# Latent heads of a streaming-encoder layer: the second pieces of long rows transposed on TensorE and split from PSUM, the first pieces' buffers placed in the chunked heads' V memory

## The chip, the cores and the metric

The kernel runs on one core of a Trainium2 chip. The metric is device time in microseconds (us), the median over runs; less is better. The engines are named as in the profile: PE (TensorE matmuls; PEld is its weight load), DVE (VectorE), ACT (ScalarE), POOL (GpSimd), SP (SyncE, which issues the DMAs here). The trace is that of one profiled execution.

## The reference

One layer over 1024 tokens of width 1024. What matters here is the attention with latent heads (eight of them), which comes after a chunked attention (eight more heads) and before the output projection and the gated MLP:

```python
def mla_attention(q, k, v):                      # q, k: 96 wide per head, v: 64 wide
    scale = Dq ** -0.5
    key_chunk = jnp.arange(S) // CHUNK           # CHUNK = 64
    def block(args):                             # Q_BLOCK = 128 queries
        qi, i = args
        s = jnp.einsum('bqhd,bkhd->bhqk', qi, k) * scale
        q_chunk = (i * Q_BLOCK + jnp.arange(Q_BLOCK)) // CHUNK
        s = jnp.where((key_chunk[None, :] <= q_chunk[:, None])[None, None], s, NEG_INF)
        p = jax.nn.softmax(s, axis=-1)
        return jnp.einsum('bhqk,bkhd->bqhd', p, v)
```

Row block i of a head (0 to 7) sees the keys of blocks 0 to i, so its probabilities are 128 x 128(i+1). The texts below number these rows 1 to 8: row n has 128n columns.

## The kernel before

Everything is fp32 in, fp32 out; products are made from pairs of a high and a low part (three matmuls for fp32r pairs in `gemm3`, L150 to L152; two fp16 halves for probabilities and V). The stages are: adaptive norm and the chunked heads' q and k, then attention, then the output projection, then the MLP (from about 752 us on). The change touches the attention stage alone, and there the latent heads, from about 430 to 680 us.

A head is handled as two units of four rows (`Unit`, `mla_unit`). A unit's `prep` makes its q page and k page in `qk_page` (L612 to L626): four PE transposes (L618) into a PSUM tile of the tag `T`, which has one buffer (`TB` = 1), then ACT writes the high part (L621 for q, L624 for k) and DVE the low part (L622, L625). The names in the trace are `mq_ps`, `mk_ps`, `mq`, `mk`.

`scores(i)` then makes one row: fp32r matmuls into one of two PSUM tiles `S` (L658, `sm`), a memset of the masked corner (L676) and the row's minimum (L677, `mm`) on DVE, the exponential with its sum on ACT (L683, `Pm`), the reciprocal and its scale on DVE (L685, L686, `rim`). Rows of more than 640 columns (rows 6, 7 and 8) are cut into a first piece of 512 columns and a second of 256, 384 or 512. For each piece POOL writes the high fp16 half into a buffer `hl` (L71), DVE the low half (L703), and SP issues a DMA transpose of both halves (L705) into `PT`. The tags `HL` and `PT` have three buffers each (`HL_BUFS`, `PT_BUFS`).

`values(i)`, three rows later (`DEPTH` = 3), multiplies the transposed halves with V (L716, `pvm`) into the PSUM tile `pv`; after four rows ACT and DVE make the output (L723, `sbm`; L724, `om`), and SP stores it.

Two things set the order of the work. The program text interleaves rows with pieces of other work ("fillers": the second latent group's q, k and V in `f_up`, and half of the output projection in `f_oca`, whose PE products are `oc` and whose loads are `cl` and `wor`), so many per row as `pace` asks for. And the scheduler reorders each engine's queue by priority: scores have an offset of 400, pieces 200, values 200. What it can't change is the order in which tiles of one tag get their buffers, which is that of the program text. The chunked heads' V lies in six buffers of the tag `v16` (`f_v`), of 2 KB a partition.

Of the kernel before, what the change touches and what calls it, by code (L numbers as in the profile page):

```python
# [12 lines left out]
F32 = mybir.dt.float32  # L13
F32R = mybir.dt.float32r
F16 = mybir.dt.float16
BF16 = mybir.dt.bfloat16
I32 = mybir.dt.int32
AF = mybir.ActivationFunctionType
# [3 lines left out]
MUL, ADD, SUB, MIN, MAX = ALU.mult, ALU.add, ALU.subtract, ALU.min, ALU.max  # L22

P = 128
# [16 lines left out]
P_BUFS, HL_BUFS, PT_BUFS, TB = 3, 3, 3, 1  # L41
# [21 lines left out]
def layer_kernel(ctx, tc, I, out):  # L63
    nc = tc.nc
    pe, act, dve, pool, sp = nc.tensor, nc.scalar, nc.vector, nc.gpsimd, nc.sync
# [4 lines left out]
    def scale_pool(o, i, s):  # L70
        pool.tensor_scalar(o, i, s, 1.0, op0=MUL, op1=MUL)  # L71
# [24 lines left out]
    ident = cst.tile([P, P], F32, name="ident")  # L96
# [27 lines left out]
    apg = att_pg.__enter__()  # L124
# [5 lines left out]
    ps = psA.__enter__()  # L130
# [12 lines left out]
    def pgtile(shape, dt, name):  # L143
        return apg.tile(shape, dt, name=name, tag="pg", bufs=6)
# [91 lines left out]
    for d in range(ND):  # L236
        if d + 1 < ND:
            load_ada(d + 1)
        w = wada[d]
# [15 lines left out]
        for t in range(NT):  # L255
            h, j = divmod(t, 4)
# [74 lines left out]
    at = att.__enter__()  # L331
# [296 lines left out]
    class Unit:  # L628
# [7 lines left out]
        def scores(u, i):  # L636
# [3 lines left out]
            lo = max(0, i - 4) if u.band else 0  # L640
            n = (i - lo + 1) * P
            nm = f"{u.nm}_{i}"
            rsum = cst.tile([P, 1], F32, name=f"rs{nm}", tag="rsum", bufs=4)
            ri = cst.tile([P, 1], F32, name=f"ri{nm}", tag="ri", bufs=4)
            with tc.high_priority(offset=OFF_S):
# [17 lines left out]
                if u.band:  # L663
                    if i >= 4:
                        dve.memset(sv[64:128, 0:64], BIG)
                    w = min(n, 256)
# [11 lines left out]
                pieces = [(0, n)] if n <= 640 else [(0, 512), (512, n)]  # L678
                if n <= 640:
                    pr = at.tile([P, 640], F32, name=f"P{nm}", tag="P", bufs=P_BUFS)  # L680
                else:
                    pr = pgtile([P, 1024], F32, f"P{nm}")
                act.activation(pr[:, :n], sv, AF.Exp, bias=m[:], scale=-1.0, accum_out=rsum[:, 0:1])  # L683
            with tc.high_priority(offset=OFF_P):
                dve.reciprocal(ri[:], rsum[:, 0:1])  # L685
                dve.tensor_scalar(ri[:], ri[:], PSCALE, None, op0=MUL)  # L686
                u.pt[i] = []
                for x, (p0, p1) in enumerate(pieces):
                    w = p1 - p0
                    hl = at.tile([P, 1280], F16, name=f"hl{nm}_{x}", tag="HL", bufs=HL_BUFS)  # L690
                    pp = pr[:, p0:p1]
                    cnt[0] += 1
                    mode = (MODE_C if u.band else MODE_M)[cnt[0] % 4]
                    if mode == "2":
                        scale_pool(pp, pp, ri[:])
                        act.activation(hl[:, :w], pp, AF.Copy)
                        pool.tensor_tensor(hl[:, w:2 * w], pp, hl[:, :w], op=SUB)
                    else:
                        if mode == "1":
                            scale_pool(hl[:, :w], pp, ri[:])  # L700
                        else:
                            act.activation(hl[:, :w], pp, AF.Copy, scale=ri[:])
                        dve.scalar_tensor_tensor(hl[:, w:2 * w], pp, ri[:], hl[:, :w], op0=MUL, op1=SUB)  # L703
                    tt = at.tile([P, 10, P], F16, name=f"PT{nm}_{x}", tag="PT", bufs=PT_BUFS)
                    sp.dma_start_transpose(tt[:, :2 * w // P, :], hl[:, :2 * w])  # L705
                    u.pt[i].append((tt, lo + p0 // P, w // P))
            return sum(3 * max(107, w / 2.4) for _, _, w, _ in segs)
# [109 lines left out]
    for n in range(len(tiles) + DEPTH):  # L817
        if n < len(tiles):
            u, i = tiles[n]
# [4 lines left out]
        if n >= DEPTH:  # L824
            u, i = tiles[n - DEPTH]
# [47 lines left out]
    for t in range(NT):  # L873
        lo = gb.tile([P, 4, P], F32R, name=f"ol{t}", tag="ol", bufs=3)
# [39 lines left out]
    def split(src, nm, tag="ws"):  # L914
        w = mt(tag, [P, 2, 512], nm, F32R)
        hi_of("a", w[:, 0], src)
        lo_of("p", w[:, 1], src, w[:, 0])
        return w
# [130 lines left out]
    for h in range(2):  # L1049
# [4 lines left out]
        for j in range(NF):  # L1054
# [3 lines left out]
            w = [split(raw[:, n * 512:(n + 1) * 512], f"wds{h}_{j}{n}") for n in range(2)]  # L1058
# [93 lines left out]
```

## Time and profile before

| what | value |
|---|---|
| median of 3 runs | 1462.71 us (1461.91 to 1462.82) |
| profiled execution, its own time | 1464.36 us |
| its span | 1462.2 us, mean granted clock 0.934 |
| busy PE, PEld | 1278.0 (87%), 1058.7 (72%) |
| busy DVE, ACT, POOL | 1013.6 (69%), 611.4 (42%), 823.0 (56%) |
| DMA transposes for latent heads | 88, 3.3 us from issue to landing (median) |
| DMA transposes for chunked heads | 64, 3.2 us |
| chain that ended last | PE 39%, DMA 17%, DVE 15%, POOL 13%, issue 12% |

Busy time is the sum of an engine's instructions; the shares are averages over stages with different limits. The chain is followed back from the last instruction, at each step to what released it; "issue" is time in which an engine waited for nothing that the profile shows. In a group's row the numbers after the bar are its busy time, the mean time of one in ns, and the idle time of the engine before them with what ended it. In a row of waits they are the total, the number of times and the longest. In the table of stretches a stretch's start and end come first, then its length, each engine's busy time, PE's granted clock, the DMA engines' busy share and the rate in GB/s.

### The profile page before, as it was taken

The page shows a single profiled execution, that of the slowest core. Times are in us where ns is not written, and L with a number is a line of the kernel's source. Part 1 is how long each engine was busy: PE and PEld are TensorE (multiplying, and loading weights), DVE is VectorE, ACT ScalarE, POOL GpSimd, SP SyncE. Part 2 cuts the span into 40 slices and gives each one's busy share as a digit, 9 for nine tenths or more (in the row PEclk, how much of TensorE's full clock was granted, in tenths as well). Part 3 has the DMA queues.
Part 4 walks back from the last instruction along what each step waited for, and adds up shares of the span by engine and source line. Part 5 has one row for each costly group of instructions (what it writes and reads, how often), then busy time and mean ns, then how long its engine had stood idle before and what let it go on. Part 6 is the DMA issues. An engine that isn't in the chain of part 4 may idle for free.

```text
span 1462.2 us, 20198 instructions
## 1 busy us (share of the span) xinstructions
PE 1278.0 (87%) x6836; PEld 1058.7 (72%) x6836; DVE 1013.6 (69%) x1734; ACT 611.4 (42%) x1190; POOL 823.0 (56%) x845
## 2 busy tenths in 40 slices
PE   3859989998967788885776999999999998999997
PEld 2759878886756666664655878788888887887885
DVE  6874776476667868872476887777777777566653
ACT  4453354243455545543274434344444433332331
POOL 5263554274599954534644555566655555665662
PEclk9979987999787899996887999999999999999998
DMA  7323647455522577879611322322222244446442
GB/s 281 134 71 74 131 114 148 129 119 120 112 52 51 115 163 156 180 142 253 246 72 59 105 110 101 116 87 87 87 87 83 75 140 164 151 144 238 146 142 101
DMA packets 218595, 185.94 MB, mean 127 GB/s; under 512 B 148086, under 2 KB 183034, under 8 KB 217468
## 3 DMA queue, kind: packets, MB, share of 16 engines
q1 hardware_dynamic: 218492, 184.66, 44.5%
q8 instruction: 54, 0.88, 0.3%
q14 instruction: 49, 0.40, 0.1%
HBM read 121.17 MB, written 28.84 MB: 103 GB/s over the span
## 4 chain that ended last, share of the span: by engine, by line
PE 39%; DMA 17%; DVE 15%; POOL 13%; issue 12%; ACT 3%; SPq 1%; DVEq 0%; POOLq 0%; ACTq 0%
POOL wds L82 5%; DMA aw<-w_ada 5%; PE p L924 4%; PE p L926 4%; PE p L925 4%; DMA wu<-w_up 3%; DMA PTm<-hlm 3%; PE sc L658 2%; PE dnp L1067 2%; PE dnp L1069 2%; PE dnp L1068 2%; PE sm L658 2%; DVE adacc L243 2%; DVE aacc L430 1%; DVE u L1002 1%
## 5 line engine op out<-in xcount | busy, mean ns | idle before, releaser
L82 POOL TENSOR_TENSOR wds<-wd,wds 128x512 fp32r<-128x512 f32 x88 | 154.6, 1777 | 99.0 <-ACT wds L75 99.0
L82 POOL TENSOR_TENSOR wc<-ws,wc 128x512 fp32r<-128x512 f32 x22 | 65.4, 2972 | 137.8 <-ACT wc L75 137.8
L1057 DVE TENSOR_TENSOR wd<-wd,gmbc 128x1024 f32<-128x1024 f32 x44 | 67.5, 1533 | 80.4 <-DMA wd<-w_down 80.4
L1069 PE MATMUL dnp<-wds,g 128*128 128x512 f32 x308 | 118.4, 390 | 4.5 <-DVE g L82 4.5
L1067 PE MATMUL dnp<-wds,g 128*128 128x512 f32 x308 | 119.6, 390 | 1.9 <-DVE xo L1075 1.9
L75 ACT ACTIVATE wds<-wd 128x512 fp32r<-128x512 f32 x88 | 54.8, 624 | 157.3 <-PE dnp L1069 152.2
L1068 PE MATMUL dnp<-wds,g 128*128 128x512 f32 x308 | 119.5, 389 | 0.0
L71 POOL TENSOR_SCALAR hlm<-Pm,rim 128x512 f16<-128x512 f32 (+4 forms) x88 | 61.9, 706 | 70.1 <-DMA PTm<-hlm 55.1
L703 DVE SCALAR_TENSOR_TENSOR hlm<-Pm,rim,hlm 128x512 f16<-128x512 f32 (+4 forms) x88 | 68.0, 777 | 30.1 <-POOL hlm L71 29.7
L71 POOL TENSOR_SCALAR hlc<-Pc,ric 128x640 f16<-128x640 f32 (+2 forms) x64 | 45.3, 710 | 76.9 <-DVE ric L686 41.2
L1015 DVE TENSOR_TENSOR ws<-wu,wu 128x512 f32<-128x512 f32 x22 | 30.7, 1396 | 76.2 <-DMA wu<-w_up 76.2
L82 DVE TENSOR_TENSOR g<-gr,g 128x512 fp32r<-128x512 f32 x44 | 71.9, 1635 | 11.5 <-ACT g L75 11.5
L1001 DVE SCALAR_TENSOR_TENSOR u<-c,pk,u 128x1023 f32<-128x1023 f32 x44 | 77.4, 1765 | 2.0 <-ACT u L1000 2.0
L1036 ACT ACTIVATE u<-u 128x1024 f32<-128x1024 f32 x22 | 23.4, 1063 | 132.1 <-DVE u L1002 132.1
L683 ACT ACTIVATE Pc<-sc,mc 128x640 f32<-128x640 f32 (+2 forms) x64 | 42.1, 659 | 82.5 <-DVE mc L673 62.0
L658 PE MATMUL sm<-mk,mq 96*128 96x512 f32 (+3 forms) x288 | 68.9, 372 | 7.9 <-ACT Pm L683 7.3
L1000 ACT ACTIVATE u<-c,pk 128x1024 f32<-128x1024 f32 x44 | 52.3, 1236 | 56.2 <-DVE c L1032 56.2
L716 PE MATMUL pvm<-PTm,vt 128*128 128x128 f16 x576 | 50.5, 242 | 28.8 <-DMA PTm<-hlm 24.3
L658 PE MATMUL sc<-k,q 64*128 64x512 f32 (+3 forms) x288 | 70.3, 372 | 4.9 <-ACT Pc L683 3.0
L430 DVE SCALAR_TENSOR_TENSOR aacc<-aw,cs,aacc 128x256 f32<-128x256 f32 x84 | 44.9, 535 | 40.6 <-DMA aw<-w_ada 40.0
L716 PEld LDWEIGHTS <-vt 128*128 128x128 f16 x576 | 41.1, 109 | 41.7 <-issue 38.3
L1069 PEld LDWEIGHTS dnp<-wds,g 128*128 128x128 f32 x308 | 57.8, 188 | 17.7 <-DVE g L82 5.7
(368 smaller groups left out, 4342.0 us busy)
## 6 DMA issues: line engine op xcount, KB each, us to landing
wu<-w_up SPq DMA_DIRECT2D x44, 512.0 KB, 4.3
wd<-w_down SPq DMA_DIRECT2D x44, 512.0 KB, 4.7
aw<-w_ada SPq DMA_DIRECT2D x96, 128.0 KB, 2.3
g_d<-u SPq DMA_DIRECT2D x22, 512.0 KB, 2.6
gr<-g_d SPq DMA_DIRECT2D x44, 256.0 KB, 3.7
x<-x SPq DMA_DIRECT2D x16, 512.0 KB, 8.3
adaw<-w_ada_a SPq DMA_DIRECT2D x8, 1024.0 KB, 5.5
wq_r<-w_qk SPq DMA_DIRECT2D x32, 128.0 KB, 2.6
```

What stands on the lines that cost most here:

```text
L71: pool.tensor_scalar(o, i, s, 1.0, op0=MUL, op1=MUL)
L82: (pool if eng == "p" else dve).tensor_tensor(o, i, f32(hi), op=SUB)
L430: dve.scalar_tensor_tensor(acc[:], w[:], cs[:, k:k + 1], acc[:], op0=MUL, op1=ADD)
L658: last = pe.matmul(s[:, c:c + w], qpg[rs_, a, q], kpgs[kh][rs_, b, ko:ko + w], start=(a == 0 and b == 0), stop=(a == 1))
L703: dve.scalar_tensor_tensor(hl[:, w:2 * w], pp, ri[:], hl[:, :w], op0=MUL, op1=SUB)
L716: last = pe.matmul(u.pv[:, c], u.vst(j), mov, start=(x == 0), stop=(x == len(todo) - 1))
L924: pe.matmul(pt, sh, pg[:, 0], start=(k == 0), stop=False)
L1001: dve.scalar_tensor_tensor(u[:, 1:], c[:, :S - 1], pk[:, cv + 1:cv + 2], u[:, 1:], op0=MUL, op1=ADD)
L1057: dve.tensor_tensor(raw[:], raw[:], gmbc[:], op=MUL)
L1067: pe.matmul(pts[t][n], sh, w[n][:, 0], start=(j == 0), stop=False)
L1068: pe.matmul(pts[t][n], sh, w[n][:, 1], start=False, stop=False)
L1069: pe.matmul(pts[t][n], sl, w[n][:, 0], start=False, stop=(j == NF - 1))
```

## The change

For rows 6, 7 and 8 of the latent heads the second piece no longer goes through `hl` and a DMA transpose. POOL scales the piece in place in fp32, PE transposes it in blocks of 128x128 into a tile of tag `T`, ACT copies the tile to the fp16 high half in `PT`, and DVE writes the low half as the difference of the tile and that half. The first piece of such a row keeps its way, but its `hl` and its `PT` come from the tag `v16`. Rows of up to 640 columns, and all rows of the chunked heads, are as before.

```diff
                 for x, (p0, p1) in enumerate(pieces):
                     w = p1 - p0
-                    hl = at.tile([P, 1280], F16, name=f"hl{nm}_{x}", tag="HL", bufs=HL_BUFS)
+                    if x:
+
+                        tt = at.tile([P, 10, P], F16, name=f"PT{nm}_{x}", tag="PT", bufs=PT_BUFS)
+                        nk = w // P
+                        scale_pool(pr[:, p0:p1], pr[:, p0:p1], ri[:])
+                        tp = ps.tile([P, 512], F32, name=f"tp{nm}", tag="T", bufs=TB)
+                        for j in range(nk):
+                            pe.transpose(tp[:, j * P:(j + 1) * P], pr[:, p0 + j * P:p0 + (j + 1) * P], ident[:])
+                        th = tt[:, :nk, :].rearrange("p a b -> p (a b)")
+                        act.activation(th, tp[:, :w], AF.Copy)
+                        dve.tensor_tensor(tt[:, nk:2 * nk, :].rearrange("p a b -> p (a b)"), tp[:, :w], th, op=SUB)
+                        u.pt[i].append((tt, lo + p0 // P, nk))
+                        continue
+                    if len(pieces) > 1:
+                        hl = apg.tile([P, 1024], F16, name=f"hl{nm}_{x}", tag="v16", bufs=6)
+                    else:
+                        hl = at.tile([P, 1280], F16, name=f"hl{nm}_{x}", tag="HL", bufs=HL_BUFS)
...
-                    tt = at.tile([P, 10, P], F16, name=f"PT{nm}_{x}", tag="PT", bufs=PT_BUFS)
+                    if len(pieces) > 1:
+                        tt = apg.tile([P, 8, P], F16, name=f"PT{nm}_{x}", tag="v16", bufs=6)
+                    else:
+                        tt = at.tile([P, 10, P], F16, name=f"PT{nm}_{x}", tag="PT", bufs=PT_BUFS)
                     sp.dma_start_transpose(tt[:, :2 * w // P, :], hl[:, :2 * w])
```

## The prediction

> **What bounds the kernel now.** First the cores' line: one core, mean granted clock 0.934, span 1462.2 us; the profiled execution itself took 1464.36, so 2.16 us lie around the span, and the execution is 1.65 above the median 1462.71. The change touches only rows of the latent heads, so the second view is the table of stretches, cut at the first exponential of each of the eight latent heads (L683, a row's 128 columns wide one):
>
> ```profile
> core 0: us, PE busy (x) PEld busy (x) DVE busy (x) ACT busy (x) POOL busy (x), PEclk, DMA share, GB/s
> 432.70:475.20 42.50, 30.32 (x157) 25.09 (x157) 31.63 (x87) 23.41 (x59) 40.34 (x74) 0.76 0.24 48
> 475.20:503.10 27.90, 20.25 (x126) 15.73 (x125) 24.20 (x63) 18.12 (x43) 26.78 (x46) 0.90 0.54 116
> 503.10:533.60 30.50, 27.63 (x166) 21.84 (x166) 21.79 (x48) 14.63 (x31) 21.01 (x26) 0.92 0.70 156
> 533.60:565.60 32.00, 25.44 (x174) 20.69 (x173) 21.54 (x53) 14.56 (x32) 12.99 (x17) 0.90 0.75 141
> 565.60:590.60 25.00, 21.41 (x149) 17.06 (x148) 21.08 (x52) 13.94 (x31) 14.15 (x15) 0.93 0.81 184
> 590.60:615.20 24.60, 20.66 (x149) 16.41 (x150) 19.40 (x49) 13.69 (x28) 12.36 (x14) 1.00 0.81 165
> 615.20:639.80 24.60, 21.35 (x150) 16.96 (x149) 20.13 (x48) 11.50 (x27) 10.69 (x14) 0.93 0.75 156
> 639.80:680.00 40.20, 24.69 (x193) 20.16 (x190) 21.57 (x52) 14.29 (x31) 16.94 (x20) 0.81 0.76 167
> ```
>
> Heads 0 and 1 are bound by POOL (40.34 of 42.50, 26.78 of 27.90), which still prepares the second group's q and k. From head 2 on no engine is full: in heads 4 to 6 PE is busy for 84 to 87% and DVE for 79 to 84%, with DMA at 0.75 to 0.81. Third, the waits between 500 and 680 us:
>
> ```profile
> POOL hlm L71 <- DMA PTm<-hlm: 55.1, 33, 4.3
> ...
> DVE hlm L703 <- POOL hlm L71: 24.9, 25, 3.3
> PE pvm L716 <- DMA PTm<-hlm: 18.4, 15, 2.5
> ```
>
> That is the ring of three `HL` buffers: POOL may not write the next piece before a DMA transpose has read an old one. This is what the change relieves. Fourth, ACT's timeline at a change of head, from the last row's exponential (1024 wide) to the next head's first (128 wide):
>
> ```profile
> 636.82 1.12 ACT L683 ACTIVATE Pm<-sm,mm 128x1024 f32<-128x1024 f32 x1 [2.36 <-DVE mm L677]
> ...
> 639.79 0.36 ACT L683 ACTIVATE Pm<-sm,mm 128x128 f32<-128x128 f32 x1
> ```
>
> Read so for all heads, the stage from 432.7 to the last head's output at 680.2 splits into "runs" (first to last exponential of a head: 36.7, 24.9, 29.5, 30.8, 21.7, 20.4, 21.6, 19.6, sum 205), "turns" (last exponential to the next head's first: 5.8, 3.0, 1.0, 1.1, 3.3, 4.2, 3.0, sum 21) and a tail (659.4 to 680.2, 20.8): 247. The turns are short because the next head's q and k pages go through the one bank `T` while the old head is still running. Last, the prices, by line and shape within the stage (the other prices below are rows of the same view), and from the chain four PE transposes:
>
> ```profile
> L703 DVE SCALAR_TENSOR_TENSOR hlm<-Pm,rim,hlm 128x512 f16<-128x512 f32 x40 | 34.1, 853 | 17.3 <-POOL hlm L71 17.2
> L71 POOL TENSOR_SCALAR hlm<-Pm,rim 128x512 f16<-128x512 f32 x40 | 30.4, 759 | 39.4 <-DMA PTm<-hlm 30.3 <-DVE rim L686 4.2 <-DVE sm L676 2.4
> ...
> L624 ACT ACTIVATE mk<-mk_ps,gk_m 96x512 fp32r<-96x512 f32 x15 | 10.2, 679 | 10.9 <-PE mk_ps L618 10.9
> L622 DVE TENSOR_TENSOR mq<-mq_ps,mq 96x512 fp32r<-96x512 f32 x15 | 10.2, 677 | 0.1
> ...
> L683 ACT ACTIVATE Pm<-sm,mm 128x1024 f32<-128x1024 f32 x8 | 8.9, 1107 | 3.2 <-DVE mm L677 3.2
> L621 ACT ACTIVATE mq<-mq_ps 96x512 fp32r<-96x512 f32 x15 | 8.8, 587 | 6.0 <-PE sm L658 5.3 <-PE mq_ps L618 0.5
> ```
>
> ```profile
> 612.20 0.44 PE mk_ps L618 x4
> ```
>
> **What is removed.** 24 of 88 DMA transposes (rows 6, 7, 8 of eight heads), with 18 of each head's 72 blocks of 128x128, a quarter; SP gets back 24 issues of at least 1.17 us, some 30 us of its queue, none of it on the path by itself. 24 subtractions on DVE go (539, 886 and 853 ns for 256, 384 and 512 columns, 2.3 us a head).
>
> **What is added, a head.** Nine PE transposes, 0.11 each: 1.0 us, in PE's idle time. Three ACT copies out of PSUM (512 wide: 0.594 as L610; less for the narrower ones, about 1.5 in all) on an engine that is 47 to 56% busy in heads 4 to 6: hidden except in the turn. Three subtractions from PSUM on DVE; no such form is in the trace, the nearest is L622 at 0.677 for 512 columns, so 1.7 a head against the 2.3 removed. POOL's scaling of the second piece stays, but writes fp32 in place; no such form is in the stage, and the bounds are the f16 form's median over all widths, 0.69, and its longest, 1.24; I take 0.76, its mean at 512 columns. DVE thus does some 0.6 less a head: nothing of it shows while the turns set the pace.
>
> **What is moved.** The first pieces' buffers move to the six `v16` slots, the chunked heads' V. Their last reader is a product at 408.5 us, the first long row comes after 455: no wait. Three rows of first pieces then fit there, and `HL` holds rows 1 to 5 alone, so POOL's 55.1 us of waiting ends. It was cover for nothing: what is late next is DVE.
>
> **The new wait.** `T` has one buffer (TB = 1), given out in program order. The transposes of row 8's second piece stand in `scores` before the next head's `prep`. So the next head's q page may not be transposed before DVE has read row 8's second piece. The order of the built program shows just that: in every one of the seven turns PE now has row 7 and 8's transposes, products, q page, row 8's products, k page, and only then the next head's scores, where before the q page stood in front of row 4 or 5. Queued behind the q page on PE are row 8's products and everything of the next head; on ACT and DVE the q and k halves.
>
> The turn then has two chains. By the bank: exponential and its sum 1.107 + 0.195; reciprocal and scale 0.153 + 0.146; POOL 0.76; four transposes 0.45; ACT 0.59; DVE 0.68; q page 0.45 + 0.59 + 0.68; k page 0.45 + 0.68 + 0.73; row 1's scores 0.41, memset and minimum 0.40: 8.5, and some 14 handoffs of about 0.07 (as the timeline shows between a producer's end and its consumer's start): 9.4. By row 8's products, which PE has in front of the k page: 1.30 + 0.30; POOL's two pieces 1.52; DVE 0.85; DMA transpose 3.3 (the page's median); 16 products 1.0; ACT 0.68 for the head's output and 0.68 for the k page; DVE 0.73; scores and minimum 0.81: 11.2, with handoffs 12. The longer one decides: 12 for six turns. In the first, POOL's queue also has some 19 us of the second group's preparation between row 8 and the next head's row 1; POOL is full there anyway, so moved work is done earlier, and I put 15 (from 12, if the queue drains freely, to 18).
>
> The runs get shorter, since nothing of the old head is left in them and no `HL` wait: DVE has there 5.7 of minima, 0.8 of memsets, 2.1 of reciprocals, 4.6 of low parts, 1.4 for the second pages, 0.74 for an output, 0.45 for row 6's second piece: 15.8, the lower bound. At the 80% at which DVE ran in heads 4 to 6 it is 19.7, the upper. Following head 5 step by step in the new order, row prices as above, I get its eight exponentials at 1.1, 2.3, 4.4, 7.7, 10.3, 13.1, 16.2 and 19.3 after the k page is ready, a run of 18: rows 3 and 4 wait on DVE behind the second pages' low parts, row 5 for the second k page, rows 7 and 8 for a score buffer and for DVE. Head 0 stays at 36.7 (POOL), head 1 goes from 24.9 to 22 (POOL's remainder is smaller). The tail is the turn's second chain up to the output: 1.3 + 0.3 + 1.52 + 0.85 + 3.3 + 1.0 + 0.68 + 0.74 and handoffs: 10.4 instead of 20.8.
>
> Sum: runs 36.7 + 22 + 6 x 18 = 166.7; turns 15 + 6 x 12 = 87; tail 10.4: 264, against 247: 17 more. Runs give 38, the tail 10, turns take 66. On the span that is 1479, on the execution's own time 1481.4, on the median 1479.5. With all terms at their lower ends (turn 9.4 and 12, run 16, head 1 at 20) the stage is 231, 16 less; at their upper ends (turn 13 and 18, run 19.7, head 1 at 25) 286, 39 more.
>
> The Trainium skill's Perfetto Trace Analysis, section Matmuls, says that independent matmul groups should rotate through several PSUM banks, so that reading one out overlaps the next group; this change does the reverse, and by that rule the turn is the price; no run so far shows a PSUM tile shared in this way. Its page VectorE: DVE Perf Modes, section The three transpose paths, gives 390 ns for TensorE against 1309 ns for the DMA crossbar, for one 128x128 bf16 block, and advises TensorE; the rows here agree in direction (0.11 a block on PE, 3.3 for a DMA transpose of up to ten), and that is the first rival's rule.
>
> **The rivals.**
> Faster: DMA is the true bound. For: DMA share 0.70 to 0.81 from head 2 on, 55.1 + 18.4 us of waiting for transposes, a quarter of the blocks gone. If transposes then land in their shortest 2.4 instead of 3.3, the second chain is 11, and if ACT, DVE and PE take q's page without waiting the turn is 9.4; with runs at 16 the stage is 231, so 1446; with turns of 10.5 and runs of 16.5, 242, so 1457. It decides from a run and turn of under 27.2 together (30 less the 17 spread over six heads). Against: from head 4 on the head takes 24.6 with PE and DVE at 80% and more, so little is left to win, and the bank's order is fixed in the program.
>
> Much slower: PE's clock. The granted clock is 0.76 in head 0 and 0.81 in the last stretch, where PE is busy 71 and 61%, and 0.90 to 1.00 in the others, busy 73 to 91%. If it falls to 0.76 in the latent stage, PE's 3 us of each turn and the 5 us of scores in a run that nothing covers get 20% longer, 1.6 a head, 13 in all; and where an output (`om`) stands before row 7's or 8's minimum on DVE, as in three heads beside head 5, a run gains about 2: together with the 17 some 36 more, 1499.
>
> No change: runs at 16.5 and turns at 10.8 would cancel, 1462.7; that is one point of the spread, not a mechanism.
>
> The change not doing what it says: `v16` still held, or the schedule putting the pages early again. The first is excluded by the 46 us between, the second by the order.
>
> **Numbers.** What a measurement here can tell from no change is about 0.2%, 3 us. My forecast (turns decide, 3 to 33 more) has 0.68, much slower 0.10, faster 0.16, no change 0.06. The range 1456 to 1500 leaves out about 0.1 below and half of much slower and a little of the forecast above.
>
> **What would show it.** Right: turns of 10 to 13 us on ACT's timeline, runs of 16 to 20, the wait of POOL for `PTm<-hlm` nearly gone, waits of PE for DVE at the q and k pages up by several us a head, tail near 10. Wrong: turns under 9 (the bank's chain overlaps more than I see), or runs that stay above 20 (DVE's order costs what `HL` cost), or DMA landings well under 3.

## The result, and the profile after

| what | before | after |
|---|---|---|
| median, runs side by side on one chip (4 each) | 1462.45 us | 1515.73 us (1515.28 to 1516.25) |
| ratio, 95% interval | | 1.0352 (1.0337 to 1.0366) |
| span of the profiled execution, granted clock | 1462.2 us, 0.934 | 1513.5 us, 0.922 |
| latent stage, first exponential to last output | 432.7 to 680.2: 247.6 | 434.1 to 727.8: 293.7 |
| runs, sum of eight | 205.2 | 163.4 |
| turns, sum of seven | 21.5 | 119.2 |
| tail | 20.8 | 11.1 |

The kernel is 3.5% slower. Of the 51.3 us that the span grew, 46.1 lie in the latent stage, 1.4 before it and 3.7 behind it. The runs became 42 shorter, the tail 10, and the turns 98 longer. First the table of stretches of the changed kernel, cut as before at the first exponential of a head:

```profile
core 0: us, PE busy (x) PEld busy (x) DVE busy (x) ACT busy (x) POOL busy (x), PEclk, DMA share, GB/s
434.10:487.50 53.40, 36.74 (x213) 29.34 (x213) 39.31 (x101) 29.63 (x74) 50.91 (x96) 0.87 0.24 51
487.50:530.50 43.00, 33.53 (x186) 25.05 (x187) 25.67 (x57) 20.23 (x44) 30.67 (x43) 0.88 0.54 129
530.50:562.80 32.30, 22.81 (x154) 17.83 (x153) 19.59 (x49) 13.78 (x31) 11.43 (x14) 0.89 0.45 96
...
596.80:631.20 34.40, 26.76 (x157) 21.27 (x157) 19.08 (x50) 14.17 (x30) 9.65 (x13) 0.81 0.41 91
...
663.10:696.90 33.80, 25.95 (x158) 20.84 (x158) 19.25 (x49) 14.17 (x29) 9.76 (x13) 0.80 0.42 92
```

Heads 4 to 6 took 24.6 to 25.0 before and take 31.9 to 34.4 now. Nothing is full in them: DVE 19 of 34, PE 26 of 34, POOL 10 of 34, and the DMA share fell from 0.75 to 0.81 to 0.41 to 0.42. A stage in which every engine has slack and which is longer than before points to a chain of waits. The waits from 500 us to the stage's end:

```profile
POOL hlm L71 <- DVE rim L686: 46.0, 15, 12.9
...
POOL hlm L71 <- ACT Pm L683: 33.5, 7, 10.9
...
PE pvm L735 <- DMA PTm<-hlm: 23.9, 22, 2.8
...
DVE hlm L719 <- POOL hlm L71: 9.4, 14, 1.3
```

Of the 55.1 us in which POOL waited for a buffer of `HL` 1.1 are left, as forecast. In their place POOL waits 46.0 and 33.5 us for a row to scale, up to 12.9 at a time: it stands idle through the turn. ACT's timeline of one turn (head 4's last row to head 5's first) shows what fills it:

```profile
614.82 1.11 ACT L683 ACTIVATE Pm<-sm,mm 128x1024 f32<-128x1024 f32 x1 [0.85 <-DVE rim L685]
...
621.37 0.49 ACT L699 ACTIVATE PTm<-tpm 128x384 f16<-128x384 f32 x1 [1.35 <-PE tpm L697]
...
623.26 0.60 ACT L699 ACTIVATE PTm<-tpm 128x512 f16<-128x512 f32 x1 [0.19 <-PE tpm L697]
625.23 0.68 ACT L742 ACTIVATE sbm<-pvm,vabm 64x512 f32<-64x512 f32 x1 [1.36 <-PE pvm L735]
625.93 0.59 ACT L621 ACTIVATE mq<-mq_ps 96x512 fp32r<-96x512 f32 x1
628.02 0.68 ACT L624 ACTIVATE mk<-mk_ps,gk_m 96x512 fp32r<-96x512 f32 x1 [1.49 <-PE mk_ps L618]
631.19 0.37 ACT L683 ACTIVATE Pm<-sm,mm 128x128 f32<-128x128 f32 x1 [2.48 <-DVE mm L677]
```

Row 7's second piece (384 wide), row 8's (512), the q page and the k page follow each other through the one bank `T`, and only then can the next head's first row exist: 16.4 us from exponential to exponential. PE's timeline of the same turn has the same order:

```profile
620.49 0.85 PE L697 MATMUL tpm<-ident,Pm 128*128 128x128 f32 x3
...
622.60 0.63 PE L697 MATMUL tpm<-ident,Pm 128*128 128x128 f32 x4 [0.47 <-DVE PTm L700]
...
625.02 0.60 PE L618 MATMUL mq_ps<-ident,qn 128*96 128x128 f32 x4
627.34 0.64 PE L618 MATMUL mk_ps<-ident,kn 128*96 128x128 f32 x4 [1.71 <-DVE mq L622]
628.75 2.01 PE L658 MATMUL sm<-mk,mq 96*128 96x128 f32 x6 [0.78 <-ACT mk L624]
```

And the prices of the new operations, by line and shape:

```profile
L71 POOL TENSOR_SCALAR Pm<-Pm,rim 128x512 f32<-128x512 f32 x8 | 6.4, 802 | 2.2 <-ACT PTm L699 1.3 <-DVE rim L686 1.0
...
L700 DVE TENSOR_TENSOR PTm<-tpm,PTm 128x512 f16<-128x512 f32 x8 | 5.5, 688 | 8.3 <-ACT PTm L699 8.2
...
L699 ACT ACTIVATE PTm<-tpm 128x512 f16<-128x512 f32 x8 | 4.7, 592 | 5.9 <-PE tpm L697 5.9
```

They were forecast at 0.76, 0.68 and 0.594. These prices were right within 6%; the turn was not.

### The profile page after: what moved, and what is told of

Same layout as the page of the kernel before. It is cut to its first block, busy times and chain, and to the rows that moved or that the text cites. A ratio compares the mean times of both kernels' runs of the same rounds, so it can differ in the third digit from the quotient of the medians.

```text
span 1513.5 us, 20279 instructions
## 1 busy us (share of the span) xinstructions
PE 1304.6 (86%) x6908; PEld 1077.8 (71%) x6908; DVE 1012.7 (67%) x1734; ACT 624.0 (41%) x1214; POOL 815.7 (54%) x845
## 4 chain that ended last, share of the span: by engine, by line
PE 25%; POOL 10%; DVE 8%; issue 8%; DMA 6%; ACT 1%; DVEq 0%; SPq 0%; POOLq 0%; ACTq 0%
POOL wds L82 5%; PE p L943 4%; PE p L945 4%; PE p L944 4%; DMA wu<-w_up 3%; PE dnp L1086 2%; PE dnp L1088 2%; PE dnp L1087 2%; DVE u L1021 1%; PE sm L658 1%; DVE ws L1034 1%; DVE u L1020 1%; POOL wf L82 1%; POOL we L82 1%; DMA PTm<-hlm 1%
## 5 line engine op out<-in xcount | busy, mean ns | idle before, releaser
L1076 DVE TENSOR_TENSOR wd<-wd,gmbc 128x1024 f32<-128x1024 f32 x44 | 65.1, 1479 | 83.3 <-DMA wd<-w_down 77.9
L71 POOL TENSOR_SCALAR hlm<-Pm,rim 128x128 f16<-128x128 f32 (+3 forms) x64 | 43.4, 679 | 101.6 <-DVE rim L686 46.0
L658 PE MATMUL sm<-mk,mq 96*128 96x512 f32 (+3 forms) x288 | 73.8, 385 | 14.9 <-ACT mk L624 6.0
L735 PE MATMUL pvm<-PTm,vt 128*128 128x128 f16 x576 | 54.0, 251 | 35.0 <-DMA PTm<-hlm 30.1
L735 PEld LDWEIGHTS <-vt 128*128 128x128 f16 x576 | 44.7, 114 | 48.5 <-issue 44.5
L82 DVE TENSOR_TENSOR g<-gr,g 128x512 fp32r<-128x512 f32 x44 | 71.9, 1637 | 10.7 <-ACT g L75 10.6
L658 PEld LDWEIGHTS sm<-mk,mq 96*128 96x128 f32 x288 | 51.2, 206 | 29.3 <-ACT mk L624 9.4
```

What stands on the lines that cost most here:

```text
L82: (pool if eng == "p" else dve).tensor_tensor(o, i, f32(hi), op=SUB)
L658: last = pe.matmul(s[:, c:c + w], qpg[rs_, a, q], kpgs[kh][rs_, b, ko:ko + w], start=(a == 0 and b == 0), stop=(a == 1))
L735: last = pe.matmul(u.pv[:, c], u.vst(j), mov, start=(x == 0), stop=(x == len(todo) - 1))
L1076: dve.tensor_tensor(raw[:], raw[:], gmbc[:], op=MUL)
```

## The experiments

In what follows "turns" is the sum of seven, "turns 2 to 6" the mean of the last five (the first two also hold the second group's preparation). In the changed kernel the turns are 19.7, 23.9, 13.9, 15.5, 16.4, 13.8 and 16.0; turns 2 to 6: 15.1. Each ratio is to the kernel before on the same chip; the kernel before took 1462.5 to 1468.1 us, by the chip. Turns, runs, tails and stages are read from one profiled execution of each kernel. How well they repeat is shown by the one kernel that was profiled twice (v16 with earlier loads, below): stage 235.8 and 235.7, the rest of the span behind it 785.2 and 787.0, the time to its start 438.2 and 433.0. "The rest" below is the span from the stage's last output on.

### Is it the bank and its order?

**Pages first.**

```diff
-                u.prep()
+                if u not in early:
+                    u.prep()
+            if not u.band and i == 5 and n + 3 < len(tiles):
+                w = tiles[n + 3][0]          # next latent head
+                need(w.need); w.prep(); early.append(w)
             pace(u.scores(i), ...)
```

> The changed kernel, with one thing different: the next latent head's first q and k pages are made (and so get the bank T) before row 6's scores of the running head, so T is given out as next q page, next k page, row 6, 7, 8's second pieces. All splits from PSUM, all PE transposes and the v16 buffers stay. Bank-order theory: the seven turns (last exponential of a head to the next head's first), 13.8 to 23.9 us each and 119 in all in the changed kernel, fall to 2 to 6 each, 30 in all; the pieces of rows 6 to 8 move into the next head's run, which grows from 18 to some 22 to 25, and the second q page now waits for row 8's piece; stage from 294 to about 245 us, the time near 1465. Rival, the splits themselves (ACT and DVE work from PSUM): time stays within 10 of 1516, since the same splits are made. Rival, PE's clock: granted clock in the stage stays 0.77 to 0.90, and the time stays above 1500.

Measured: 1484.61 us, ratio 1.0150 (1.0123 to 1.0177). Turns 14.9 in all, runs 239.0, tail 10.9, stage 264.8. The turns went from 119 to 15 with every split, transpose and buffer in place, so the order in which `T` is given out made them. The time near 1465 and the stage near 245 that were expected did not come: the runs grew by 76, more than the 32 to 56 expected. The pieces are now worked off in the next head's run, and its second pages stand behind row 8's piece instead, so a part of the wait moved and did not go: the stage is still 17 longer than before.

**Second pieces in another bank.**

```diff
-tp = ps.tile([P, 512], F32, name=f"tp{nm}", tag="T", bufs=TB)
+tp = ps.tile([P, 512], F32, name=f"tp{nm}", tag="mm", bufs=2)
```

> The changed kernel, with the second pieces' transposes written into the tag mm (two buffers, shared with the filler products) instead of T; text order unchanged. Bank-order theory: the next head's pages no longer stand behind row 8's second piece, so they are made during the old head's run as before the change; turns fall to 3 to 6, 30 in all, runs to 19 to 24, stage about 240 to 250, time 1460 to 1475. New cost: filler products and pieces share two banks. Rival, splits themselves or PE's clock: time above 1500, since both stay. If e1 and e2 agree within 10, the bank and its order are the cause, not PE's order alone.

Measured: 1473.95 us, ratio 1.0079 (1.0055 to 1.0102). Turns 20.6, runs 202.7, stage 245.4. ACT goes from one head's last row to the next head's first in 1.8, without a split between them:

```profile
606.73 1.12 ACT L683 ACTIVATE Pm<-sm,mm 128x1024 f32<-128x1024 f32 x1 [0.16 <-DVE rim L686]
...
608.51 0.37 ACT L683 ACTIVATE Pm<-sm,mm 128x128 f32<-128x128 f32 x1 [0.57 <-POOL hlm L71]
```

The stage is back to that of before (247.6), with nine PE transposes and three splits a head still in it. In the stage the cost of the change is the shared bank, not the way over PE. The time is not back: the stage began 4.0 later than before, and the rest is 789.6 us long, 7.6 more. The rest is taken up below.

**Two banks for T.**

```diff
-P_BUFS, HL_BUFS, PT_BUFS, TB = 3, 3, 3, 1
+P_BUFS, HL_BUFS, PT_BUFS, TB = 3, 3, 3, 2
-tag="mm", bufs=2      (all uses)
+tag="mm", bufs=1
```

> The changed kernel, with two buffers for T and one for mm (PSUM is full, so the second bank is taken from the filler products). Read are the turns of heads 2 to 7; the time also holds what the single filler bank costs elsewhere, in the chunked heads too. If the bank sets the turn: the next head's q page takes the bank of row 7's piece while row 8's is split, so the q page's 2.4 and its wait of 0.9 leave the chain: turns 2 to 6 at 11 to 12.5 instead of 15.1. If products ahead in PE's order decide: turns above 14.

Measured: turns 2 to 6 at 12.4, 10.1, 12.2, 13.5 and 12.1, mean 12.1, 3.1 less than with one bank and inside the expected 11 to 12.5. (The time, 1551.18 in one run, holds what a single filler bank costs: the latent stage began at 478.7 instead of 434.1.) PE's timeline of the shortest of these turns (10.1, from 634.9 on):

```profile
638.25 0.66 PE L697 MATMUL tpm<-ident,Pm 128*128 128x128 f32 x4 [1.63 <-POOL Pm L71]
638.75 0.60 PE L618 MATMUL mq_ps<-ident,qn 128*96 128x128 f32 x4
...
643.67 0.94 PE L658 MATMUL sm<-mk,mq 96*128 96x128 f32 x6
```

The q page is transposed 0.5 after row 8's piece, where with one bank it came 2.4 after it. The Trainium skill's Perfetto Trace Analysis, section Matmuls, has this as its rule: independent matmul groups rotate through different PSUM banks, so that reading one out overlaps the next. The trace agrees in direction. The 3.1 us a turn are not the bank's alone: this kernel also has one filler bank less, and PE's granted clock was 0.72 to 1.00 in these turns, where with one bank it was 0.62 to 0.78.

### The parts of the change by themselves

**v16 alone**: the kernel before, with only the first pieces' buffers moved.

```diff
-hl = at.tile([P, 1280], F16, name=f"hl{nm}_{x}", tag="HL", bufs=HL_BUFS)
+if len(pieces) > 1 and x == 0:
+    hl = apg.tile([P, 1024], F16, name=f"hl{nm}_{x}", tag="v16", bufs=6)
+else:
+    hl = at.tile([P, 1280], F16, name=f"hl{nm}_{x}", tag="HL", bufs=HL_BUFS)
 # the same for tt (PT)
```

> The kernel before, with only the first pieces' buffers of rows 6 to 8 in v16; the second pieces keep HL and their DMA transposes. It tells what relief of the HL ring alone brings. If the ring paced heads 2 and 3 (30 us a head, POOL waiting 55 us for transposes): POOL's wait falls below 25 us and the stage by 5 to 15, time 1448 to 1458. If the transposes' DMA time paces them (DMA share 0.70 to 0.81): within 4 of 1462. If v16 itself does harm (rival for the changed kernel): above 1470.

Measured: 1462.45 us, ratio 0.9987 (0.9967 to 1.0007). The buffers do no harm. POOL's wait for `HL` fell from 55.1 to 31.7 us, less than expected, and the stage from 247.6 to 238.9. The 1448 to 1458 expected did not come: the stage began 3.0 later, and the rest is 790.4 instead of 782.0, so in the profiled execution the gain is given back. (That execution, 1466.78, was the longest of ten; the interval of the ratio leaves room for a gain of 0.3%.)

**PE alone**: the changed kernel, with the first pieces back in `HL` and `PT`.

```diff
-if len(pieces) > 1:
-    hl = apg.tile([P, 1024], F16, name=f"hl{nm}_{x}", tag="v16", bufs=6)
-else:
-    hl = at.tile([P, 1280], F16, name=f"hl{nm}_{x}", tag="HL", bufs=HL_BUFS)
+hl = at.tile([P, 1280], F16, name=f"hl{nm}_{x}", tag="HL", bufs=HL_BUFS)
 # the same for tt (PT)
```

> The changed kernel, with the first pieces' buffers back in HL and PT; only the second pieces go over PE and PSUM. Bank-order theory: turns stay 13 to 24, 119 in all; HL now takes three pieces of rows 6 to 8 as well, of which the turn's cover is enough: runs 18 to 20; time 1512 to 1525. Rival, v16 does the harm: time 1460 to 1480.

Measured: 1517.04 us, ratio 1.0374 (1.0346 to 1.0402); turns 129.5, runs 160.1, tail 14.9. The whole loss lies in this half of the change.

### Why is a turn 15 and not 12?

**No filler**: no filler is paced into the latent heads once the second group is made.

```diff
-pace(u.scores(i), R_CA if u.band else R_MLA)
+pace(u.scores(i), R_CA if u.band else 0 if "up1" in done else R_MLA)
 # the same for u.values(i)
```

> The changed kernel, with no filler work paced into the latent heads once the second group's q, k and V are made: the output projection's half (oc) comes after the last head instead. What is read is the turns, not the time (the products moved to the end cost 25 to 45 us there). If filler products that stand in PE's queue ahead of row 7's and 8's transposes are what made turns longer than the forecast 12: the turn from head 1 to 2 falls from 23.9 to 13 to 15, turns 2 to 6 from a mean of 15.1 to 12 to 13. If only the two uses of the one bank in series and the order of the pages made them longer: 23.9 still falls, but turns 2 to 6 stay within 1 of 15.1. Clock rival: if the lower granted clock in turns comes from PE's idle time, it falls below 0.7 there, and the turns get no shorter.

Measured: turns 19.6, 17.8, 11.5, 16.5, 16.1, 15.9, 16.5; turns 2 to 6: 15.3. The turn from head 1 to 2 owed 6.1 of its 23.9 to filler (45 `oc` products stood in PE's queue ahead of the k page there). Of the later ones the first fell by 2.4, and the other four moved by -0.3 to 2.1, so filler did not make their length. The clock in these five turns was 0.54 to 0.85. The turn of 11.5 (head 2 to 3) shows that one bank does not force 15: row 7's piece was out of the bank by the time POOL had scaled row 8's, whose transposes began 3.2 after the exponential. In the other four they began 5.1 to 7.4 after it.

**Second piece first**: the pieces of rows 6 to 8 in the other order.

```diff
-for x, (p0, p1) in enumerate(pieces):
+for x, (p0, p1) in list(enumerate(pieces))[::-1]:
```

> The changed kernel, with the two pieces of rows 6 to 8 handled in the other order: the second piece (over PE and T) first, the first piece (DMA transpose) behind it. It tells which chain sets the turn. In the changed kernel the bank T comes free 5.4 to 9.8 after row 8's exponential starts (turns 2 to 6, mean 7.6), and 7.5 more pass to the next head's first exponential. Bank chain: T comes free 0.7 to 1.5 earlier, turns 2 to 6 fall from a mean of 15.1 to 13.6 to 14.4, time 1505 to 1512; the tail grows by 0.7 to 1.1, since the DMA starts later. Products and DMA chain (the forecast's longer one): turns 2 to 6 grow by 0.7 to 1.1 with the tail, time 1518 to 1525.

Measured: 1518.47 us, ratio 1.0355 (1.0313 to 1.0397); turns 2 to 6: 15.4, tail 14.3. Inconclusive: its four runs spread from 1510 to 1522, `T` came free 7.6 after row 8's exponential, as before, the turns moved by less than the 0.7 that either theory asked for, and the tail grew by 3.2, three times what was expected.

**Row 8 alone in T**: rows 6 and 7 in `mm`.

```diff
-tag="T", bufs=TB)
+tag="T" if i == 7 else "mm", bufs=TB if i == 7 else 2)
```

> The changed kernel, with row 6's and 7's second pieces transposed into the tag mm, and row 8's alone into T: it takes away the two uses of T in series, and leaves the next head's pages behind row 8. If the wait of row 8's transposes for row 7's split is what the forecast missed: T comes free 1.5 to 2.5 earlier, turns 2 to 6 at 12.6 to 13.6, time 1500 to 1508. Rival: PE's own queue (products that wait for DMA, filler in front of row 8's transposes) held them anyway: turns within 0.8 of 15.1, or longer where filler now stands in front, time 1512 or more. Bank-order theory as a whole: in either case turns stay above 11, since the pages still stand behind row 8.

Measured: 1546.75 us, ratio 1.0539 (1.0491 to 1.0587); turn 0 46.4, turns 2 to 6: 16.5. Up to twelve `oc` products and row 7's products now stood ahead of row 8's transposes on PE, and `T` came free at 8.6 instead of 7.6. The run mixes two effects, and was repeated below without filler and without the DMA-fed products. What makes its turn 0 so long was not separated.

**No DMA-fed products**: the products of row 7's and 8's first pieces are left out.

```diff
-for tt, lo, nk in u.pt[i]
+for tt, lo, nk in (u.pt[i][1:] if len(u.pt[i]) > 1 and i > 5 else u.pt[i])
```

> The changed kernel, leaving out the products of row 7's and row 8's first pieces (16 of 30 products in the turn, those that wait for a DMA transpose); pieces, transposes, splits, T's order, fillers and the pages are as they were. Read are the turns. Theory now: the forecast held the bank's chain and the products' chain to run side by side, and took the longer; in PE's in-order queue they stand in series (row 7's products, waiting for their DMA, ahead of row 8's transposes or of the q page). Then turns 2 to 6 fall from a mean of 15.1 to 10.5 to 12.5 (the bank's chain of 9.4 and PE's slower pages and scores, +1 to +3). Rival: the chain's own steps (two splits in series, pages, scores) are what is slow: turns stay at 13.5 to 15. Since DVE, POOL and the DMAs still do all their work, no other load is taken off.

Measured: turns 17.0, 14.7, 14.2, 13.1, 13.7 for 2 to 6, mean 14.5 instead of 15.1. Four of the five became 0.7 to 2.3 shorter, the first 3.1 longer. The theory that the products' chain stands in series with the bank's and makes the missing time fell: on the mean it is worth 0.6, not 2.6 to 4.6.

**Neither DMA-fed products nor filler**: the two edits together.

```diff
+for tt, lo, nk in (u.pt[i][1:] if len(u.pt[i]) > 1 and i > 5 else u.pt[i])
...
+pace(u.scores(i), R_CA if u.band else 0 if "up1" in done else R_MLA)
```

> The same (no products of row 7's and 8's first pieces), and no filler paced into the latent heads after the second group's q, k and V (it follows the last head, so the time is long and not read). Nothing that waits for a DMA and nothing foreign is left in PE's queue in turns 2 to 6: what remains is the bank's chain alone. Forecast of that chain: 9.4. If it is 9 to 10.5, the chain was costed right and the error is PE's queue alone; if 11 to 13, the steps themselves were costed 2 to 3 too low (row 7's use of T ahead of row 8's, pages and scores at the lower clock); turn 1 falls from 23.9 to 14 to 17.

Measured: turns 14.5, 13.8, 14.9, 14.7, 15.2, mean 14.6; turn 1 fell to 17.7. So with neither filler nor DMA-fed products in PE's queue the bank's chain takes 14.6, where I had 9.4: in these turns it was not the shorter of the two chains. PE's timeline of one of these turns (row 8's exponential at 605.8, the next head's first at 620.7):

```profile
608.64 0.85 PE L697 MATMUL tpm<-ident,Pm 128*128 128x128 f32 x3
...
611.49 0.63 PE L697 MATMUL tpm<-ident,Pm 128*128 128x128 f32 x4 [0.83 <-DVE PTm L700]
...
614.11 1.06 PE L618 MATMUL mq_ps<-ident,qn 128*96 128x128 f32 x4
616.57 1.09 PE L618 MATMUL mk_ps<-ident,kn 128*96 128x128 f32 x4 [1.41 <-DVE mq L622]
618.44 2.01 PE L658 MATMUL sm<-mk,mq 96*128 96x128 f32 x6 [0.77 <-ACT mk L624]
```

Two things are read here. Row 8's transposes wait for DVE to have read row 7's piece: the bank is used four times in a turn, not three. And four transposes take 1.06 and six score matmuls 2.01, where with two banks the same instructions took 0.60 and 0.94 (the lines above). PE's granted clock from 618.4 to 620.5 is 0.50. My row of 0.44 from before is no measure of this: it comes from the chain, which counts an instruction only up to the next one's start, and the timeline of before has 0.60 for the same four transposes.

**The same, with row 8 alone in T.**

```diff
 # the two edits above, and
-tag="T", bufs=TB)
+tag="T" if i == 7 else "mm", bufs=TB if i == 7 else 2)
```

> The run without the DMA-fed products and without filler (turns 2 to 6: mean 14.6, T free 7.6 after row 8's exponential starts, 7.0 from there to the next head's first exponential), and in addition rows 6's and 7's second pieces in mm, row 8's alone in T. With nothing foreign in PE's queue this takes away only the use of T by row 7. If the two uses in series are the missed term: T free at 5.2 to 6, turns 2 to 6 at 12.5 to 13.3. If POOL (which scales row 7's piece before row 8's) and DVE hold row 8 anyway: T free at 7 or later, turns above 14.

Measured: turns 13.4, 13.7, 14.3, 13.9, 13.6 for 2 to 6, mean 13.8 (turn 0 is 42.8, as long as in the run with row 8 alone in `T`); `T` free at 6.7 instead of 7.6. Row 7's use of the bank costs about 0.9 a turn, about half of what was expected. POOL's scaling of row 8's second piece ends 3.7 after the exponential's start, since POOL first has pieces of row 7 or row 8's own first piece. In two of the five turns row 8's transposes start within 0.1 of that end; in the other three they start 0.6, 1.1 and 1.8 after it, behind products and row 7's transposes in PE's queue.

### A version that beats both

The stage with v16 alone was 8.7 shorter than before, and nothing came of it. In the three profiles of before, mm alone and v16 alone the last split of the output projection's weights (`wo`) on DVE ends at 696.0, 703.9 and 699.7, and the MLP's first product begins at 779.3, 787.2 and 782.9: 83.3, 83.3 and 83.2 later. This speaks for the rest waiting for these loads, not for the stage. They stand behind the filler in the program, in two shared buffers. The interval is not fixed, though: in the five profiles below with v16 and at most row 8's piece over PE it is 80.0 to 82.2, and in the two whose last split came only 10.4 and 5.5 after the stage it is 86.5 and 88.6, so there something else came last.

**v16, and half of wo loaded earlier.**

```diff
 # v16 alone, and in f_oca's second half, behind each second product:
+                if n and t % 2:
+                    wo[0] += load_wo(t // 2, 0, "a", "p", t // 2 + 1)
 ...
-    wo = [load_wo(0, n, "a", "v" if n else "p") for n in range(2)]
+    wo[1] = load_wo(0, 1, "a", "v")
```

> The kernel before with the first pieces' buffers in v16 (as in the run of v16 alone), and the first four of the eight last weight tiles of the output projection (wo, for rows 0 to 3 of the left half) loaded and split during the second half of the filler product, not behind it. In the run of v16 alone the latent stage ended 5.6 earlier than in the kernel before, yet the span was 2.8 longer: the last split of wo came at 699.7 instead of 696.0, 25.1 after the stage's last output instead of 15.8. Theory that these loads gave the gain back: last split at most 17 after the last output, the rest of the span 782 or less, time 1452 to 1459. Rival, the rest is bound by other loads (attention outputs and x): rest of the span stays at 790, time 1462.

Measured: 1461.30 against 1468.05 us, ratio 0.9948 (0.9923 to 0.9972). Stage 235.8, last split at 696.4, MLP's first product at 776.8. The 6.8 us gained lie in what was expected against the 1462.5 of the first chip (3.5 to 10.5); the time itself, on a chip on which the kernel before is longer, lies above 1452 to 1459. The step did not come as expected: the last split was still 22.4 after the last output, not 17, and the rest 785.2, not 782. By the program text the second four weights need buffers that the filler's last products free; no run tests that.

**The same loads with mm** (second pieces over PE in `mm`, v16), and **the control** (kernel before, same loads). Both have this edit, on the mm kernel above and on the kernel before:

```diff
+                if n and t % 2:
+                    wo[0] += load_wo(t // 2, 0, "a", "p", t // 2 + 1)
```

> The changed kernel with the second pieces' transposes in the tag mm, and the same earlier loads of wo. In the run with mm alone the stage took 245 us, 48 less than in the changed kernel, but the rest of the span was 789.6, 7.6 more than in the kernel before. Theory: rest falls to 782 or less, time 1462 to 1468. Rival (other loads bound the rest): 1474.

> The kernel before with the same earlier loads of wo and nothing else: the control. Its rest of the span is 782.0 already, the shortest seen is 777.0: time 1457 to 1463, and less gain than in the other two.

Measured: with mm 1467.99, ratio 1.0010 (0.9994 to 1.0027): the rest fell from 789.6 to 783.3, near the expected 782, but the stage took 250.3 instead of 245.4 (the profiled execution, 1471.62, was the longest of ten). Control 1467.64, ratio 1.0002 (0.9988 to 1.0017): the rest 775.9, the stage 5.2 longer. Loads alone bring nothing and v16 alone brings nothing that was measurable; together they bring 0.5%. Against v16 with the same loads (stage 235.8), sending the second pieces over PE, even in another bank, makes the stage 14.5 longer.

**Row 8 alone over PE** (v16 and the earlier loads, with row 8's second piece over PE and `mm`, rows 6 and 7 by DMA).

```diff
+if x and i == 7:
+    ...        # scale in place, PE transposes into mm, ACT and DVE split
+    continue
```

> A version from the findings: v16 for the first pieces, the earlier wo loads, and of the second pieces only row 8's over PE, into a filler bank (mm), rows 6 and 7 by DMA as before. Against the version with v16 and early wo alone (0.9948 of the kernel before): if the DMA transposes still pace the heads (DMA share 0.73 to 0.86), 3 to 8 us less, 0.990 to 0.994; if a filler bank held by a piece costs as much (as with mm for all pieces, stage 250 against 236), no gain, 0.995 to 1.002.

Measured: 1468.07 against 1466.70, ratio 0.9998 (0.9979 to 1.0017), stage 248.4, 12.6 more than with v16 and the loads alone. Row 8's piece over PE gives their gain back; that the filler bank held by the piece is the cost was expected, but no run separates it.

**A faster pace of the filler** (v16 and the earlier loads, with the edit below), and **both paces once more**.

```diff
-R_CA, R_MLA = 1.9, 0.5
+R_CA, R_MLA = 1.9, 0.6
```

> The best version so far (kernel before, first pieces in v16, wo loaded earlier; 0.9948 of the kernel before), with the filler's pace in the latent heads raised from 0.5 to 0.6, so that the output projection's half is done before the last head and the remaining wo loads start sooner. In that version the last wo split came 22.4 after the stage's last output. If these loads still bound the rest: 2 to 6 less, 0.990 to 0.994. If the added filler lengthens heads 2 to 6 by as much (PE is 76 to 90% busy there): 0.994 to 0.998.

> The version with v16 for the first pieces and the earlier wo loads, once more with more rounds: 0.9948 of the kernel before in the first comparison (0.9923 to 0.9972). If it is a gain it stays at 0.993 to 0.997.

> The same with the filler's pace at 0.6: 0.9977 in the first comparison (0.9954 to 1.0), though its stage was the shortest of all, 230 us. If the pace helps, it lies below the version at 0.5 on the same chip; if what is gained in the stage is given back in the projection behind it, within 0.002 of it.

Measured: pace 0.6, first 0.9977 (0.9954 to 1.0), again 0.9978 (0.9961 to 0.9995); pace 0.5 again 1459.97 against 1466.11, 0.9953 (0.9930 to 0.9976). Pace 0.6 has the shortest stage of all (230.1 and 229.5), and its rest is 797.4 and 795.8: the last split of `wo` came at 697.3 in the second of its profiles, 33.4 after the last output. What is gained in the stage is given back behind it. The version with v16 and the earlier loads, at pace 0.5, beats the kernel before by about 0.5% in both comparisons (both intervals lie below 1), and so the changed kernel.

## Why the prediction was right or wrong

The sign was right, with the mechanism that was put down as likeliest: one bank, given out in program order, puts the next head's pages behind row 8's second piece. The size was not: 1479 with a range to 1500, and 1515.7 measured. The stage was forecast at 264 and took 293.7; of the 29.6 missing, the turns are 32.2 (87 forecast, 119.2 measured), the runs -3.3 (166.7 and 163.4), the tail 0.7 (10.4 and 11.1). The failed step is the turn's term: none of the seven turns lies in the 10 to 13 that the prediction gave as a sign of being right.

**What was right.** Removing the `HL` wait brought runs of 18 (18.5, 18.4, 18.0, 18.1 and 17.8 for heads 2 to 6). That their sum came within 3.3 is partly luck: heads 0 and 1 took 33.7 and 19.0, each 3.0 less than forecast, and head 7 took 19.8, 1.8 more. The prices of the new operations stood. `v16` did no harm. The pages did stand behind row 8, and no gain of DMA showed: the share fell by half and the heads grew. One sign did not come: PE's waits for DVE at the q and k pages were to grow by several us a head, and PE's idle time put down to DVE just ahead of them is 5.7 in the whole stage, against 8.2 before.

**What was wrong in the turn.** I had two chains side by side, 9.4 by the bank and 12 by row 8's products, and took the longer. The bank's chain is the one that decides, and without filler and DMA-fed products it still takes 14.6. By its steps (us after row 8's exponential starts, mean of turns 2 to 6; the forecast column adds up the prediction's prices and spreads its handoffs evenly):

| step | forecast | after | no filler, no DMA-fed products | and row 7 out of T |
|---|---|---|---|---|
| POOL has scaled row 8's piece | 2.6 | 3.5 | 3.8 | 3.7 |
| PE starts row 8's transposes | 2.7 | 5.2 | 5.5 | 4.4 |
| T is free (DVE's half is written) | 4.6 | 7.6 | 7.6 | 6.7 |
| q page starts on PE | 4.6 | 8.6 | 8.2 | 7.3 |
| q page's low half is written | 6.5 | 10.9 | 10.6 | 9.7 |
| k page's low half is written | 8.6 | 13.7 | 13.1 | 12.2 |
| next head's first exponential | 9.4 | 15.1 | 14.6 | 13.8 |

- Up to T being free, 3.0 were missed. POOL has row 7's pieces or row 8's own first piece before row 8's second (0.9 to 1.2); row 7's transposes are ahead in the same bank (0.9 by the last of these runs); the piece's own split takes 2.1 to 2.4 instead of 1.9. I had counted row 8's piece, the q page and the k page, and not row 7's.
- From there on 2.7 were missed. The q page starts on PE behind products, 0.6 to 1.0 after T is free. From its start to the next head's first exponential I had 4.8, and it took 6.5. Four transposes take 0.60 in the timeline, where I had 0.45 by the chain's row, twice; two rows' scores are interleaved, where I had one row's; and the head's output (`sbm`, `om`) stands in front of the q page's halves on ACT and DVE, as ACT's timeline above shows at 625.23. PE's clock is the smaller part: without filler and DMA-fed products this stretch took 6.6 in the three turns with all page transposes at 1.06 to 1.09 and scores at 2.01, and 6.2 in the two with page transposes at 0.60 to 0.64, so I estimate it at 0.5 a turn.
- Filler and DMA-fed products in PE's queue are 0.5 in the mean of turns 2 to 6 (15.1 against 14.6) and 6 in the turn from head 1 to 2, where I had put 12 and 23.9 came. From head 0 to 1 it was 19.7 against 15.
- "In every one of the seven turns" the q page ahead of row 8's products was not so: in two, from head 4 to 5 and from 6 to 7, both pages come after them, and these are the longest of turns 2 to 6 (16.4 and 16.0).

**The rivals.** The faster one (DMA bounds) was wrong for this change: with v16 in both, the stage took 245.4 with the second pieces over PE in `mm` and 238.9 with all of them by DMA, so taking DMA transposes away gained nothing. "Much slower" had the right direction and a small part of the cause: PE's clock does fall to half in parts of the turn, but by the estimate above that is some 0.5 of the 5.2 by which the bank's chain was missed (9.4 forecast, 14.6 measured).

**What stays open.** The steps of the table are read from one execution each, and their parts were not all tested one by one: the order on POOL, the head's output on ACT and DVE and the clock are read from the traces. Why row 8's transposes began so much earlier in one turn without filler (11.5) than in the others (15.9 to 16.5) is not settled, nor why the tail grew by 3.2 with the pieces' order reversed.

## What to carry to other kernels

A buffer with one slot serialises all its users in program order, also across the boundary of an outer loop: list every user between the last use of one iteration and the first of the next (here four, not three), and price the whole list as one chain. Such a chain is exposed at a boundary, where the engines have nothing else: price its steps from the start of one instruction to the end of it, not by rows that stop where the next one starts, and add what stands ahead in each engine's queue. And when a stage gets shorter, look at what the next stage waits for: here the loads of its weights, and not only the stage, seem to set when it began.

## What the runs showed of the hardware

PE's granted clock changed within a head, and a run's length hardly followed it. Two stretches, the run of head 4 and the turn behind it; first the kernel without filler in the latent heads, then the changed kernel:

```profile
587.50:605.10 17.60, 15.49 (x59) 11.80 (x57) 11.59 (x35) 7.16 (x17) 4.09 (x7) 0.55 0.23 44
605.10:621.30 16.20, 10.01 (x78) 8.38 (x77) 7.55 (x17) 4.55 (x9) 3.02 (x4) 0.76 0.42 80
```

```profile
596.80:614.80 18.00, 14.52 (x74) 11.26 (x75) 12.11 (x35) 8.67 (x20) 5.35 (x8) 0.90 0.39 85
614.80:631.20 16.40, 12.24 (x83) 10.00 (x82) 6.97 (x16) 5.50 (x10) 4.30 (x5) 0.71 0.44 97
```

In the run without filler the clock is 0.55 instead of 0.90, PE's busy time is longer, 15.49 against 14.52, though it ran fewer matmuls, and the run still takes 17.6 against 18.0: PE does not set the length of this run. In the turn PE again had less to do without filler, but the clock is higher, 0.76 against 0.71, so the clock does not simply follow the amount of work. Within the changed kernel's turn the clock is 1.00 from 625.0 to 627.5, where the q page's four transposes take 0.60, and 0.50 from 628.7 to 631.2, where the six score matmuls take 2.01 (0.94 with two banks). The Trainium skill's TensorE: Matmul & The Clock Gate, section Part 1: The HAM clock gate, says that the array runs at half or at full clock, by how busy it has lately been. The trace agrees as to the two rates, with ratios of 2.1 for the scores (2.01 to 0.94) and 1.8 for the transposes (1.06 to 0.60); what decides between them no run here shows. The same page of the Trainium skill, section HAM oscillation, gives "no PE-idle gaps" of over some 3.4 us as the abstract rule against falling back to the half clock; here the longest gap of PE in the turn shown was 1.95 us, and the half clock came all the same.
